# Rooms for expert weights reused in order of use, the split of x on VectorE, and splits behind the norm

## The chip, the cores and the metric

The kernel runs on one core of a Trainium2 chip. The metric is the device time of one execution in microseconds (us). Besides the executions that are only timed, one was taken with a profile; all durations below come from that one.

## The reference

The reference takes a sequence of 256 tokens of width 1024 in fp32 through two blocks of one kind, one block of another and a tail. Each of the three blocks ends in a mixture of 16 experts, of which a router picks two for each token. Cut to what matters here:

```
for l in range(2):                       # first kind of block
    h = concat(gla(x @ w_in), sgu(x @ w_in)) @ w_out
    x = layer_norm(ALPHA * x + h)
    h = cross_attention(x, mem)          # wq, wk, wv, wo
    x = layer_norm(ALPHA * x + h)        # the norm ahead of the router
    h = grouped_moe(x)
    x = layer_norm(ALPHA * x + h)
x = second_mixer(x)                      # attention and a scan
h = rms_norm(x)
x = x + hier_moe(h)
out = tail(x, p)                         # a gate, a projection of p, a norm

def moe(h):                              # both kinds, apart from the router
    out = 0
    for e in range(16):
        he = silu(h @ w_gate[e]) * (h @ w_up[e])      # 1024 -> 512
        out += combine[:, e] * (he @ w_down[e])       # 512 -> 1024
```

## The kernel before, in words

**Precision.** fp32 operands of most products are split in two parts: a high part (`xsh`, `whl`, `xTh`; a copy to the type fp32r on ScalarE, line 98) and a low part (`xsl`, `xTl`; the operand minus its high part, line 78 on VectorE). Experts' weights go to TensorE as they are.

**The norm ahead of the router** (`before_moe`). It works through the two halves of 128 tokens each (`tt` 0 and 1), in step with the projection that fills `x`. For each half: statistics and `rs` (line 103 on VectorE, then a power on GpSimd, line 104), turned pieces `zT` and the router's products `q`, the logits `lg`, the normalised `x` (`normal`), its high part `xsh` (`high`) and its low part `xsl` (`low`, line 360). `low` is a subtraction of 128x1024 on GpSimd. In the third block the normalised rows go to a tile `h`, and `rs` comes from squares summed on ScalarE. For the first two blocks a multiplication and an addition of gain and bias remain for each half (`finish`, four operations `x<-x,vec` on VectorE); `vec` is the tile that holds gain and bias.

**Routing and gathering** (`moe`). From the logits come the chosen experts (`sel`), each token's place in its expert's list (`pp` on TensorE, then `pos`), and matrices `Dm` of zeros and ones (`slots`, a comparison on VectorE: two of 128x256 for experts 0 to 3, then three of 128x512 for the others). `gath` multiplies `xsh` and `xsl` with `Dm`, 16 products each, into the tokens of four experts; `XG` is the copy out of PSUM, half of the pieces on ScalarE and half on VectorE. Then eight pairs of experts follow. In pair i TensorE runs gate (`gu`, 32 matmuls), up (`gu`), `dn` of pair i-1 (32 matmuls), and between these the sums `ysum`, two small gathers and two turns (`dtp`, `gut`). `mid` holds a pair's hidden values. The last pair's `dn` stands alone behind it.

**Weights and their rooms.** Each half of an expert's matrix is 1 MB and one DMA on SyncE's queue, written in program order (`expert_load`, line 214): per block 96 loads of four kinds' rooms. Four loads in a row are gate (or up, or down) of one pair: first half of expert 0, first half of expert 1, second half of expert 0, second half of expert 1. A load waits until the room it goes to has been read by TensorE; SyncE works in order, so what is behind it waits too. SyncE also has at most eight of these loads under way: each waits for the eighth before it.

Rooms are tiles of four pools: `raw` (7), `hl` (6), `t8` (9, shared with `Dm`, `XG`, `mid` and other activations) and `vec` (1). Before, the first pass takes n rooms of `t8`, then 7 `raw`, 6 `hl` and `vec` (n, called `flex`, is 4, 5 and 4 in the three blocks); later loads go round over the 7 `raw` and 6 `hl` alone. So the first load of the second round (load number 18, 19 and 18, counted from 0) takes the first `raw` room, which holds part of the first pair's up weights. `preload` issues the first 7+n loads while the stages ahead of the experts still run.

**The rest of what the change touches.** `rsqrt` has its first step on GpSimd unless `near` is set; `layer_norm` calls it without. `ahead` issues the loads of the next stage's weights at the end of a block, and splits the first few of them at once; `an` counts both. In the third block `fill` places the small projection of the tail (`ple_load` at the head, `ple_turn` with `ptp` in pair 0, `ple_proj` with 24 matmuls `plp` in pair 6). The instructions' order on each engine is fixed when the program is built, by a list scheduler that follows the program's order and the priorities given by `urgent` and `after`.

Of the kernel before, what the change touches and what calls it, by code (L numbers as in the profile page):

```python
# [6 lines left out]
F32 = mybir.dt.float32  # L7
# [12 lines left out]
CAP = 64  # L20
# [2 lines left out]


class Net:
    def __init__(self, tc, aps, cap=CAP, fallback=True, layers=2, bufs=(7, 6, 9, 2), flex=(4, 5, 4), late=2,
                 hp=("ln", "xm"), ao=1, plat=6, an=((2, 4), (3, 5), 3)):
        self.hp = hp
        self.ao = ao
        self.plat = plat  # L30
        self.an = an
        self.late = late
        self.flex = flex
        self.early = {}
# [158 lines left out]
    def preload(self, i, Wg, Wu, Wd):  # L193


        n = self.flex[i]
        self.rooms = ["t8"] * n + ["raw"] * self.NRAW + ["hl"] * self.NHL + ["vec"]
        self.loaded = 0
        todo = [(w, e, h) for p in range(2) for w in (0, 1) for h in range(2) for e in (2 * p, 2 * p + 1)]
        self.experts = {}  # L200
        for key in todo[:self.NRAW + n]:
            self.experts[key] = self.expert_load((Wg, Wu, Wd), *key)

    def expert_load(self, W, w, e, h):
        if self.loaded < len(self.rooms):
            room = self.rooms[self.loaded]
        else:
            m = (self.loaded - len(self.rooms)) % (self.NRAW + self.NHL)
            room = "raw" if m < self.NRAW else "hl"
        self.loaded += 1  # L210
        k, f = (8, 512) if w < 2 else (4, 1024)
        n = {"raw": self.NRAW, "hl": self.NHL, "t8": self.NT8, "vec": 1}[room]
        raw = self.sb.tile([128, k // 2, f], F32, tag=room, name="we", bufs=n)
        self.tc.keep_in_program_order(self.nc.sync.dma_start(
            raw, W[w][e].rearrange("(p k) f -> p k f", k=k)[:, h * (k // 2):(h + 1) * (k // 2), :]))
        return raw
# [64 lines left out]
    def layer_norm(self, x, l, i, at_once=False):  # L281
# [13 lines left out]
        def steps(tt, c, A):  # L295
# [14 lines left out]
            if at_once:  # L310
                self.ts(mv[:, 0:1], st[:, 0, 0:1], st[:, 0, 1:2], -1.0 / D, OP.add, OP.mult)
                tmp["first"] = self.ts(mv[:, 1:2], mv[:, 0:1], 0.03125, None, OP.mult).ins
                ss = self.sm("ss", [128, 1])
                self.act(r[1][:, :, tt * 128:(tt + 1) * 128], x[:, tt, :].rearrange("p (a b) -> p a b", a=KT), AF.Square,
                         scale=0.03125, bias=mv[:, 1:2], accum_out=ss)
                self.rsqrt(rs, ss, 1e-5)
            else:
                nc.vector.bn_aggr(mv, st)
                self.rsqrt(rs, mv[:, 1:2], 1e-5)
            for c in range(2):  # L320
                self.ts(o[c], o[c], mv[:, 0:1], rs, OP.add if at_once else OP.subtract, OP.mult)
                self.turn(r, x, tt, c, gb)
# [7 lines left out]
    def before_moe(self, x, rw, v, mean, keep, got):  # L330
# [26 lines left out]

        def low(tt):
            _, z, h, o = views(tt)
            nc.gpsimd.tensor_tensor(o, z, h.bitcast(F32), op=OP.subtract)  # L360

        def finish(tt):

# [7 lines left out]
        def steps(tt, c, A):  # L371
# [19 lines left out]
            if c == 0:  # L391
                if tt:
                    normal(0)
                    high(0)
                return
            rs[tt] = self.sm("rs", [128, 1])
            if mean:
# [14 lines left out]
            self.stt(lg[:, tt, :], p, rs[tt], B, OP.mult, OP.add)  # L412
            if tt == 0:
                return turned
            low(0)
            normal(1)

        def second(exp):
            with self.after(exp):
                h = high(1)  # L420
            low(1)
            if exp:
                with self.after(h):
                    self.warm()
        got.extend((lg, xs, second, (lambda: [finish(t) for t in range(2)]) if mean else None))
        return part

    def gain_cols(self, g, b=None):
# [421 lines left out]
    def moe(self, lg, xs, second, finish, gc, route, Wg, Wu, Wd, fill, source):  # L850
# [4 lines left out]
        W = Wg, Wu, Wd  # L855
        with self.urgent("rt"):
            sel, weights, exp = route(lg)
        second(exp)
# [15 lines left out]
        def gather(e, ks):  # L874
# [5 lines left out]
            with self.urgent("ga"):  # L880
# [7 lines left out]
                for k, p in ps.items():  # L888
                    for kk in (k, k + 1):
                        o, g = XG[e][:, kk], gain[:, kk:kk + 1]  # L890
                        if offset is None:
                            if kk % 2:
                                self.ts(o, p[:, kk - k], g, None, OP.mult)
                            else:
                                self.act(o, p[:, kk - k], AF.Copy, scale=g)
                        elif kk % 2:
                            self.ts(o, p[:, kk - k], g, offset[:, kk:kk + 1], OP.mult, OP.add)
                        else:
                            self.act(o, p[:, kk - k], AF.Identity, scale=g, bias=offset[:, kk:kk + 1])

        slots(0, 4, slice(0, 1))
        slots(0, 4, slice(1, 2))
        gather(0, (0, 2, 4, 6))
        for e in (4, 8, 12):
            last = slots(e, 4)
        gate = weights()
        if finish:
            with self.after(last.ins):
# [500 lines left out]
    def body(self, upto):  # L1409
# [94 lines left out]

        def fill(where):
            nonlocal ple
            if where == "head":
                ple = self.ple_load()
            if where == 0:
                ple = self.ple_turn(ple) + (ple,)  # L1510
            if where == self.plat:
                self.ple_proj(*ple)
# [32 lines left out]
```

## Time and profile before

| | us |
|---|---|
| median of 3 runs | 1478.57 (1477.70 to 1481.46) |
| profiled execution | 1477.46 |
| its span, first to last instruction | 1475.7 |
| TensorE busy | 1380.5 (94%) |
| VectorE busy | 631.3 (43%) |
| ScalarE busy | 505.0 (34%) |
| GpSimd busy | 80.3 (5%) |
| mean granted TensorE clock | 0.978 |

PE is TensorE's matmul side, DVE VectorE, ACT ScalarE, POOL GpSimd, SP SyncE; a `q` behind a name (SPq) is the engine's own queue of DMA issues and the like. In a timeline a row gives start, length, engine, line, operation, output and inputs, shape and count; a bracket gives how long the engine sat idle ahead of it, and what it waited for. Rows of several instructions give the time from the first one's start to the last one's end. The profiled execution lasts 1.8 us longer than its span and lies 1.1 us below the median.

### The profile page before, as it was taken

How to read it: one execution, taken by the hardware profiler on the slowest of the kernel's cores; microseconds unless marked ns; L12 is line 12 of the kernel's file. 1: busy time of each engine (PE TensorE's matmuls, PEld its weight loads, DVE VectorE, ACT ScalarE, POOL GpSimd, SP SyncE). 2: the span in 40 equal slices, each digit the busy share in tenths (PEclk: the TensorE clock that was granted, in tenths of full speed). 3: DMA queues.
4: the chain of work that ended last, by engine and by line, in shares of the span. 5: the costliest groups of instructions: out<-in, count | busy, mean ns of one | idle time of the engine just before them, and what ended most of it. 6: DMA issues, size and time to landing. Idle time of an engine off the chain costs nothing. (4 is left out here: it accounts for less than half of the span.)

```text
span 1475.7 us, 18102 instructions
## 1 busy us (share of the span) xinstructions
PE 1380.5 (94%) x7258; PEld 899.4 (61%) x7258; DVE 631.3 (43%) x1074; ACT 505.0 (34%) x784; POOL 80.3 (5%) x121
## 2 busy tenths in 40 slices
PE   8999998899988898999799998799999979999987
PEld 7889897444433686898444433499878864444335
DVE  5754754412111767763512110757676641212124
ACT  5634543111100474443211100458664440111122
POOL 2110001000000002000100000000000020000000
PEclk9999999899999999999899999899999989999998
DMA  9745428599999965328599999943534577999991
GB/s 336 273 167 179 164 87 352 203 421 421 421 419 421 341 222 173 117 98 346 203 393 420 421 421 420 352 131 117 197 120 140 204 316 294 421 421 421 418 389 44
DMA packets 101964, 421.50 MB, mean 286 GB/s; under 512 B 10676, under 2 KB 10896, under 8 KB 65008
## 3 DMA queue, kind: packets, MB, share of 16 engines
q1 hardware_dynamic: 97968, 409.17, 70.8%
q0 software_dynamic: 3904, 11.09, 2.4%
q8 instruction: 60, 0.98, 0.3%
q14 instruction: 32, 0.26, 0.0%
HBM read 419.18 MB, written 1.05 MB: 285 GB/s over the span
## 5 line engine op out<-in xcount | busy, mean ns | idle before, releaser
L64 PE MATMUL gu<-we,XG 128*64 128x512 f32 x1536 | 350.6, 596 | 3.9 <-DMA we<-in_w_gate_dram 1.7
L78 DVE TENSOR_TENSOR whl<-raw,whl 128x1024 fp32r<-128x1024 f32 (+1 forms) x210 | 241.1, 1163 | 146.9 <-ACT whl L98 138.2
L98 ACT ACTIVATE whl<-raw 128x1024 fp32r<-128x1024 f32 (+1 forms) x210 | 208.1, 1009 | 200.2 <-PE acc L64 97.6
L64 PEld LDWEIGHTS gu<-we,XG 128*64 128x64 f32 x1536 | 109.2, 137 | 210.0 <-issue 193.8
L64 PE MATMUL dn<-we,mid 128*64 128x512 f32 x768 | 181.6, 595 | 22.4 <-DMA we<-in_w_down_dram 20.3
L64 PE MATMUL acc<-whl,xTh 128*128 128x512 f32 (+2 forms) x640 | 194.4, 388 | 4.3 <-ACT xTh L98 3.4
L64 PEld LDWEIGHTS dn<-we,mid 128*64 128x64 f32 x768 | 57.8, 137 | 138.6 <-issue 94.6
L64 PEld LDWEIGHTS acc<-whl,xTh 128*128 128x128 f32 x640 | 119.9, 194 | 29.8 <-ACT xTh L98 4.0
L95 ACT ACTIVATE dh<-dn,gsl 128x512 fp32r<-128x512 f32 x42 | 28.8, 688 | 286.7 <-PE dn L64 286.7
L64 PE MATMUL facc<-xTh,whl 128*128 128x256 f32 x640 | 123.0, 288 | 1.8 <-ACT xTh L98 1.8
L64 PE MATMUL acc<-whl,xTl 128*128 128x512 f32 (+1 forms) x320 | 120.2, 385 | 0.1
L78 DVE TENSOR_TENSOR mid<-mid,gu 128x512 f32<-128x512 f32 x24 | 25.4, 1057 | 215.8 <-PE gu L64 215.8
L64 PEld LDWEIGHTS facc<-xTh,whl 128*128 128x128 f32 x640 | 102.7, 194 | 2.6 <-ACT xTh L98 2.0
L64 PE MATMUL facc<-xTl,whl 128*128 128x256 f32 x320 | 91.4, 287 | 0.0
L87 DVE SCALAR_TENSOR_TENSOR dl<-dn,gsl,dh 128x512 fp32r<-128x512 f32 x42 | 31.4, 750 | 134.6 <-ACT dh L95 132.1
L95 ACT ACTIVATE XG<-gath,gc 128x256 f32<-128x256 f32 x48 | 25.2, 535 | 134.9 <-PE gath L64 134.9
L64 PEld LDWEIGHTS acc<-whl,xTl 128*128 128x128 f32 x320 | 60.7, 193 | 12.4 <-DVE xTl L78 0.6
L92 DVE TENSOR_SCALAR XG<-gath,gc 128x256 f32<-128x256 f32 x32 | 16.9, 540 | 109.6 <-ACT XG L95 109.3
L64 PEld LDWEIGHTS facc<-xTl,whl 128*128 128x128 f32 x320 | 61.8, 193 | 0.7 <-issue 0.3
L64 PE MATMUL acc<-whl,oTh 128*128 128x512 f32 x160 | 49.5, 402 | 0.5 <-ACT oTh L98 0.5
L95 ACT ACTIVATE mid<-gu 128x512 f32<-128x512 f32 x24 | 14.3, 594 | 103.1 <-PE gu L64 103.1
L64 PEld LDWEIGHTS gath<-Dm,xsh 128*128 128x128 f32 x192 | 30.9, 222 | 28.6 <-issue 26.5
(366 smaller groups left out, 1769.8 us busy)
## 6 DMA issues: line engine op xcount, KB each, us to landing
we<-in_w_gate_dram SPq DMA_DIRECT2D x96, 1024.0 KB, 15.7
we<-in_w_up_dram SPq DMA_DIRECT2D x96, 1024.0 KB, 16.0
we<-in_w_down_dram SPq DMA_DIRECT2D x96, 1024.0 KB, 19.8
raw<-in_w_in_dram SPq DMA_DIRECT2D x38, 1024.0 KB, 8.7
raw<-in_w_out_dram SPq DMA_DIRECT2D x12, 1024.0 KB, 5.0
raw<-in_wk_x_dram SPq DMA_DIRECT2D x8, 1024.0 KB, 9.6
raw<-in_wv_x_dram SPq DMA_DIRECT2D x8, 1024.0 KB, 5.8
raw<-in_wq_x_dram SPq DMA_DIRECT2D x8, 1024.0 KB, 5.0
```

What stands on the lines that cost most here:

```text
L64: return self.nc.tensor.matmul(out, lhsT=l, rhs=r, start=start, stop=stop, skip_group_check=True)
L78: return self.nc.vector.tensor_tensor(out, a, b, op=op)
L87: return self.nc.vector.scalar_tensor_tensor(out, a, s, b, op0=op0, op1=op1, **k)
L92: return self.nc.vector.tensor_scalar(out, a, s1, s2, op0=op0, op1=op1)
L95: return self.nc.scalar.activation(out, a, f, **k)
L98: return self.nc.scalar.activation(out, a, AF.Copy)
```

## The change

Four things change.

1. *Rooms.* The first pass takes 2 `raw`, 1 `t8`, 4 `raw`, 1 `t8`, 1 `raw`, 6 `hl` and 1+t `t8`, with t (`flex`) now 1, 2 and 2: 17, 18 and 18 loads, all of them issued by `preload`. Later loads go round over 3 `raw`, `vec`, 4 `raw`, 6 `hl` and t `t8`: 15, 16 and 16 rooms. The first load of the second round now takes the room of load number 0, the first pair's first gate weights.
2. *The low part of x.* `low` is a subtraction on VectorE. `low(0)` follows `high(0)`; `low(1)` follows the second `Dm`. `finish` follows the last `XG` of the first gather, and the three large `Dm` follow the second small one.
3. *Norms.* `layer_norm` calls `rsqrt` with `near`, and no split is issued early by `ahead` (the loads are the same).
4. *The tail's projection.* `ple_load` stands in pair 5, `ple_turn` in pair 6 and `ple_proj` in pair 7.

```diff
-    def __init__(self, tc, aps, cap=CAP, fallback=True, layers=2, bufs=(7, 6, 9, 2), flex=(4, 5, 4), late=2,
-                 hp=("ln", "xm"), ao=1, plat=6, an=((2, 4), (3, 5), 3)):
+    def __init__(self, tc, aps, cap=CAP, fallback=True, layers=2, bufs=(7, 6, 9, 2), flex=(1, 2, 2), late=2,
+                 hp=("ln", "xm"), ao=1, plat=7, an=((0, 4), (0, 5), 0)):
...
-        n = self.flex[i]
-        self.rooms = ["t8"] * n + ["raw"] * self.NRAW + ["hl"] * self.NHL + ["vec"]
+        r, t = self.NRAW, self.flex[i]
+        self.rooms = ["raw"] * 2 + ["t8"] + ["raw"] * 4 + ["t8"] + ["raw"] * (r - 6) + ["hl"] * self.NHL + ["t8"] * (1 + t)
+        self.round = ["raw"] * 3 + ["vec"] + ["raw"] * (r - 3) + ["hl"] * self.NHL + ["t8"] * t
...
+        todo += [(2, e, h) for h in range(2) for e in range(2)]
...
-        for key in todo[:self.NRAW + n]:
+        for key in todo[:len(self.rooms)]:
...
-            m = (self.loaded - len(self.rooms)) % (self.NRAW + self.NHL)
-            room = "raw" if m < self.NRAW else "hl"
+        i = self.loaded
+        room = self.rooms[i] if i < len(self.rooms) else self.round[(i - len(self.rooms)) % len(self.round)]
...
-                self.rsqrt(rs, mv[:, 1:2], 1e-5)
+                self.rsqrt(rs, mv[:, 1:2], 1e-5, near=True)
...
-            nc.gpsimd.tensor_tensor(o, z, h.bitcast(F32), op=OP.subtract)
+            self.tt(o, z, h.bitcast(F32), OP.subtract)
...
                     high(0)
+                    low(0)
...
-            low(0)
             normal(1)
...
-            low(1)
...
         slots(0, 4, slice(0, 1))
-        slots(0, 4, slice(1, 2))
-        gather(0, (0, 2, 4, 6))
-        for e in (4, 8, 12):
-            last = slots(e, 4)
+        first = slots(0, 4, slice(1, 2)).ins
+        with self.after(first):
+            second[1]()
+        last = gather(0, (0, 2, 4, 6))
+        with self.after(first):
+            for e in (4, 8, 12):
+                slots(e, 4)
...
-            if where == "head":
+            if where == 5:
                 ple = self.ple_load()
-            if where == 0:
+            if where == 6:
                 ple = self.ple_turn(ple) + (ple,)
```

How the instructions move follows at three places. First VectorE in the first block, from the second half's `rs` to the first gather's copies. The rows of before, from the first `Dm` on (`den` and `gate` are the gates' norming):

```order
L78 TENSOR_TENSOR Dm<-iot,pos 128x256 x2
L78 TENSOR_TENSOR Dm<-iot,pos 128x2x256 x3
L818 RECIPROCAL den<-den 128x2
L78 TENSOR_TENSOR x<-x,vec 128x1024 x2
L78 TENSOR_TENSOR gate<-gate,den 128x32
L78 TENSOR_TENSOR x<-x,vec 128x1024 x2
L87 SCALAR_TENSOR_TENSOR go<-pos,gate 128x32
L92 TENSOR_SCALAR XG<-gath,gc 128x256
L78 TENSOR_TENSOR gparts<-gate,gparts 128x16x2
L92 TENSOR_SCALAR XG<-gath,gc 128x256 x3
```

The same stretch now:

```order
L78 TENSOR_TENSOR Dm<-iot,pos 128x256 x2
L78 TENSOR_TENSOR xsl<-x,xsh 128x1024
L78 TENSOR_TENSOR Dm<-iot,pos 128x2x256 x3
L816 RECIPROCAL den<-den 128x2
L78 TENSOR_TENSOR gate<-gate,den 128x32
L87 SCALAR_TENSOR_TENSOR go<-pos,gate 128x32
L78 TENSOR_TENSOR gparts<-gate,gparts 128x16x2
L92 TENSOR_SCALAR XG<-gath,gc 128x256 x2
L915 TENSOR_REDUCE cm<-cnt 128x1
L92 TENSOR_SCALAR XG<-gath,gc 128x256 x2
L78 TENSOR_TENSOR x<-x,vec 128x1024 x4
```

The subtraction of the second half came in behind the two small `Dm`, and the four operations of `finish` went from ahead of the copies `XG` to behind them. The first half's subtraction stands a little ahead of this, on the same engine, right behind the second half's `rs`:

```order
 L103 TENSOR_SCALAR rs<-mv 128x1
+L78 TENSOR_TENSOR xsl<-x,xsh 128x1024
+L87 SCALAR_TENSOR_TENSOR nr<-mv,rs 128x1
 L87 SCALAR_TENSOR_TENSOR lgt<-gwc,mv,q 128x16
-L87 SCALAR_TENSOR_TENSOR nr<-mv,rs 128x1
 L87 SCALAR_TENSOR_TENSOR lg<-lgt,rs,gwc 128x16
```

In the second block it stands one place later, behind `nr`, and there ScalarE has the fourth `zT` ahead of the first half's `xsh`, which was behind it. Second, ScalarE ahead of the router of the third block; `xsl,ss<-x` is the sum of squares, `re` the exponential that the gates need. Before:

```order
L95 ACTIVATE xsl,ss<-x 128x1024
L98 ACTIVATE zT<-trp 128x512
L95 ACTIVATE h_8537<-x,rs 128x1024
L98 ACTIVATE xsh<-h_8537 128x1024
L98 ACTIVATE zT<-trp 128x512 x2
L95 ACTIVATE xsl,ss<-x 128x1024
L98 ACTIVATE zT<-trp 128x512
L95 ACTIVATE h_8537<-x,rs 128x1024
L98 ACTIVATE xsh<-h_8537 128x1024
L95 ACTIVATE re<-re 128x40
L95 ACT_TABLE_LOAD
L95 ACTIVATE warm<-mhalf 128x1
```

And now:

```order
L98 ACTIVATE zT<-trp 128x512 x4
L95 ACTIVATE xsl,ss<-x 128x1024 x2
L95 ACTIVATE h_8537<-x,rs 128x1024 x2
L98 ACTIVATE xsh<-h_8537 128x1024
L95 ACTIVATE re<-re 128x40
L95 ACT_TABLE_LOAD
L95 ACTIVATE warm<-mhalf 128x1
L98 ACTIVATE xsh<-h_8537 128x1024
```

The first half's norm went behind the last `zT`, and the second `xsh` behind the table load. On VectorE of that block the first `xsl` now stands between `pos` and the first `Dm`, the second behind the last `Dm`. Third, TensorE at the end of the third block's experts, from the last pair's `dtp` on. The projection now stands there:

```order
L64 MATMUL gu<-we,XG 64x512 x16
L64 MATMUL dn<-we,mid 64x512 x16
L75 MATMUL dtp<-ident,pos 128x128 x4
L64 MATMUL plp<-whl,pT 128x512 x24
L75 MATMUL gut<-ident,mid 128x128 x4
L64 MATMUL dn<-we,mid 64x512 x16
```

`plp` came from the same place one pair earlier, ahead of the last pair's gate.

## Rows read from the trace of the kernel before

**Rows 1.** The page's head: the span, and busy time by engine.

```profile
span 1475.7 us, 18102 instructions
PE 1380.5 (94%) x7258; PEld 899.4 (61%) x7258; DVE 631.3 (43%) x1074; ACT 505.0 (34%) x784; POOL 80.3 (5%) x121
```

**Rows 2.** PE's waits by cause: us in total, times, longest.

```profile
PE dn L64 <- DMA we<-in_w_down_dram: 20.3, 17, 1.4
```

**Rows 3.** Timeline of PE: a pair's gate, the next pair's, and the blocks' ends.

```profile
338.47 7.09 PE L64 MATMUL gu<-we,XG 128*64 128x512 f32 x32
...
364.40 1.94 PE L64 MATMUL gu<-we,XG 128*64 128x512 f32 x8
...
483.88 7.12 PE L64 MATMUL dn<-we,mid 128*64 128x512 f32 x32 [0.69 <-ACT mid L98]
...
929.80 5.36 PE L64 MATMUL dn<-we,mid 128*64 128x512 f32 x22 [1.44 <-DMA we<-in_w_down_dram]
...
1391.10 4.47 PE L64 MATMUL plp<-whl,pT 128*128 128x512 f32 x18 [0.16 <-DVE dl L87]
...
1427.78 5.36 PE L64 MATMUL dn<-we,mid 128*64 128x512 f32 x22 [1.44 <-DMA we<-in_w_down_dram]
```

**Rows 4.** Stretches of 15 us: busy time by engine, clock, DMA share, GB/s.

```profile
270.00:285.00 15.00, 15.00 (x74) 5.54 (x71) 1.09 (x4) 1.05 (x2) 0.00 (x0) 1.00 0.33 118
...
435.00:450.00 15.00, 11.47 (x51) 3.96 (x52) 1.64 (x2) 1.16 (x2) 0.00 (x0) 1.00 1.01 422
```

**Rows 5.** Timeline of SP: the first load of each block's second round.

```profile
281.36 0.33 SPq L214 DMA_DIRECT2D we<-in_w_down_dram  x1
...
728.46 0.33 SPq L214 DMA_DIRECT2D we<-in_w_down_dram  x1
...
1225.80 0.33 SPq L214 DMA_DIRECT2D we<-in_w_down_dram  x1
```

**Rows 6.** Timeline of the first block's routing, all engines.

```profile
251.41 2.84 POOL L360 TENSOR_TENSOR xsl<-x,xsh 128x1024 fp32r<-128x1024 f32 x1 [3.75 <-ACT xsh L98]
251.86 0.15 DVE L103 TENSOR_SCALAR rs<-mv 128x1 f32<-128x1 f32 x1
254.22 0.54 POOL L104 TENSOR_TENSOR rs<-rs,mhalf 128x1 f32<-128x1 f32 x1
258.38 2.85 POOL L360 TENSOR_TENSOR xsl<-x,xsh 128x1024 fp32r<-128x1024 f32 x1 [3.62 <-ACT xsh L98]
261.65 3.88 PE L64 MATMUL gath<-Dm,xsh 128*128 128x256 f32 x16 [3.45 <-DVE Dm L78]
263.65 2.33 DVE L78 TENSOR_TENSOR x<-x,vec 128x1024 f32<-128x1024 f32 x2
265.33 2.48 PE L64 MATMUL gath<-Dm,xsl 128*128 128x256 f32 x16
269.52 2.80 PE L64 MATMUL gu<-we,XG 128*64 128x512 f32 x12 [0.36 <-DVE XG L92]
```

**Rows 7.** `Dm` in the first and the third block: ns min/median/max, first and last start.

```profile
L78 DVE TENSOR_TENSOR Dm<-iot,pos x5: 410/677/3041, 258.5 to 263.0; 128x512 fp32r<-128x512 f32 x3, 128x256 fp32r<-128x256 f32 x2
...
L78 DVE TENSOR_TENSOR Dm<-iot,pos x5: 416/681/683, 1207.5 to 1209.4; 128x512 fp32r<-128x512 f32 x3, 128x256 fp32r<-128x256 f32 x2
```

**Rows 8.** Timeline of the routing in the second and the third block.

```profile
701.96 0.23 DVE L87 SCALAR_TENSOR_TENSOR lg<-lgt,rs,gwc 128x16 f32<-128x16 f32 x1
...
716.60 3.65 PE L64 MATMUL gu<-we,XG 128*64 128x512 f32 x16 [0.26 <-DVE XG L92]
...
1201.94 2.04 ACT L98 ACTIVATE xsh<-h 128x1024 fp32r<-128x1024 f32 x1
...
1208.08 3.84 PE L64 MATMUL gath<-Dm,xsh 128*128 128x256 f32 x16 [0.83 <-DVE Dm L78]
...
1213.96 2.37 PE L64 MATMUL gu<-we,XG 128*64 128x512 f32 x10
```

**Rows 9.** The page's groups: a strided product on VectorE.

```profile
L78 DVE TENSOR_TENSOR mid<-mid,gu 128x512 f32<-128x512 f32 x24 | 25.4, 1057 | 215.8 <-PE gu L64 215.8
```

More of the change, by code (lines that the diff above doesn't have):

```diff
@@ L193, in preload @@
     def preload(self, i, Wg, Wu, Wd):
-        n = self.flex[i]
-        self.rooms = ["t8"] * n + ["raw"] * self.NRAW + ["hl"] * self.NHL + ["vec"]
+        r, t = self.NRAW, self.flex[i]
+        self.rooms = ["raw"] * 2 + ["t8"] + ["raw"] * 4 + ["t8"] + ["raw"] * (r - 6) + ["hl"] * self.NHL + ["t8"] * (1 + t)
+        self.round = ["raw"] * 3 + ["vec"] + ["raw"] * (r - 3) + ["hl"] * self.NHL + ["t8"] * t
         self.loaded = 0
         todo = [(w, e, h) for p in range(2) for w in (0, 1) for h in range(2) for e in (2 * p, 2 * p + 1)]
+        todo += [(2, e, h) for h in range(2) for e in range(2)]
         self.experts = {}
-        for key in todo[:self.NRAW + n]:
+        for key in todo[:len(self.rooms)]:
             self.experts[key] = self.expert_load((Wg, Wu, Wd), *key)
     def expert_load(self, W, w, e, h):
-        if self.loaded < len(self.rooms):
-            room = self.rooms[self.loaded]
-        else:
-            m = (self.loaded - len(self.rooms)) % (self.NRAW + self.NHL)
-            room = "raw" if m < self.NRAW else "hl"
+        i = self.loaded
+        room = self.rooms[i] if i < len(self.rooms) else self.round[(i - len(self.rooms)) % len(self.round)]
         self.loaded += 1
@@ L315, in steps @@
                          scale=0.03125, bias=mv[:, 1:2], accum_out=ss)
-                self.rsqrt(rs, ss, 1e-5)
+                self.rsqrt(rs, ss, 1e-5, near=True)
             else:
                 nc.vector.bn_aggr(mv, st)
-                self.rsqrt(rs, mv[:, 1:2], 1e-5)
+                self.rsqrt(rs, mv[:, 1:2], 1e-5, near=True)
             for c in range(2):
@@ L424, in second @@
                     self.warm()
-        got.extend((lg, xs, second, (lambda: [finish(t) for t in range(2)]) if mean else None))
+        got.extend((lg, xs, (second, lambda: low(1)), (lambda: [finish(t) for t in range(2)]) if mean else None))
         return part
@@ L857, in moe @@
             sel, weights, exp = route(lg)
-        second(exp)
+        second[0](exp)
         pp = self.rp([128, 2, 16], "pp")
@@ L890, in gather @@
                         o, g = XG[e][:, kk], gain[:, kk:kk + 1]
[L891 to L897, printed above, removed]
-                        else:
-                            self.act(o, p[:, kk - k], AF.Identity, scale=g, bias=offset[:, kk:kk + 1])
+                        b = None if offset is None else offset[:, kk:kk + 1]
+                        if kk % 2:
+                            last = self.ts(o, p[:, kk - k], g, b, OP.mult, None if b is None else OP.add)
+                        else:
+                            self.act(o, p[:, kk - k], AF.Copy if b is None else AF.Identity, scale=g,
+                                     **({} if b is None else {"bias": b}))
+            return last
         slots(0, 4, slice(0, 1))
-        slots(0, 4, slice(1, 2))
-        gather(0, (0, 2, 4, 6))
-        for e in (4, 8, 12):
-            last = slots(e, 4)
+        first = slots(0, 4, slice(1, 2)).ins
[5 more added lines that the diff above has]
+                slots(e, 4)
         gate = weights()
```

## The prediction

> **What bounds the kernel now.** TensorE is busy for 94% of the span [rows 1], so time can only come from its gaps or its slow stretches. The list of its waits was read first: the largest entry, 20.3 us in 17 waits, is `dn` waiting for down weights [rows 2], and it shows that the experts' stages are short of weights. How much is lost there follows from a pair's pace. Unhurried, one pair follows the other after 364.40 - 338.47 = 25.9 us [rows 3], so eight take 207.4. From the first `gu` to the end of the last `dn` the three blocks took 491.0 - 269.5 = 221.5, 935.2 - 716.6 = 218.6 and 1433.1 - 1214.0 = 219.1, the last with some 6.0 of `plp` (4.47 for 18 of its 24 matmuls) [rows 3, 6, 8]. So 14.1, 11.2 and 5.7 us are lost, 31 in all. The stretches tell why: from 270 to 285 TensorE is full while DMA brings 118 GB/s, and from 435 to 450 DMA is full at 422 GB/s while TensorE works 11.47 of 15 us [rows 4]. DMA needs 2.49 us for a load of 1 MB at that rate, 29.8 for the 12 of a pair, against 25.9 on TensorE; it lives on its lead, and stands idle at the beginning, where the lead could be built. The cause of that is the row of SP: the first load of the second round is issued at 281.36, 728.46 and 1225.80 [rows 5], each time 11.8 to 11.9 us behind the first `gu`, when the first half of the pair's up weights has been read.
>
> The other gaps lie in the routing, where everything waits in a chain; the timelines were read for it [rows 6 to 8].
>
> **The change part by part: the start of the experts.** *First block.* (a) GpSimd's first `xsl` (2.84) stands from 251.41 to 254.25, and the power that makes `rs`, whose input was ready at 252.01, comes right behind it at 254.22 [rows 6]. Now VectorE does that subtraction behind `rs`. Its length is not shown. The lower bound is 1.17, a contiguous operation of this size (2.33 for two `x<-x,vec` [rows 6]); the upper 2.1, twice the strided product of 512 columns at 1.06 [rows 9]. I take 1.8, nearer the strided row, since ScalarE too takes 2.04 for `xsh` in this layout [rows 8]. It ends at 253.8, with the power done beside it: 0.5 us sooner than before, between 1.1 sooner and 0.2 later. (b) The second `xsl` on GpSimd starts at 258.38, and the first `Dm` (start 258.5) takes 3.04 us instead of 0.41, the length that the other one of its form has [rows 6, 7]. In the third block, with no subtraction beside it, the longest `Dm` is 0.68 [rows 7]. So 2.63 go. The second subtraction now follows two `Dm` of 0.41 and has 3.88 us of `gath<-Dm,xsh` to hide behind; if that cover were gone it would cost its 1.8. (c) `gath` ends at 267.81 and `gu` begins 1.71 later, behind a copy `XG` on VectorE that stood behind `finish` (four `x<-x,vec`, two of them from 263.65) [rows 6]. Third block, no `finish`: `gu` follows the copies much sooner. I take 1.2 for this, of at most 1.6. `finish` then runs under the first `gu`; it frees `vec` some 6 us after the start, which is ahead of the fourth load of the second round, the one that needs it. Sum 0.5 + 2.6 + 1.2 = 4.3 sooner, from 3.2 to 5.3.
>
> *Second block.* (b) and (c) are the same, 2.6 and 1.2 to 1.5. But ScalarE there makes the first `xsh` behind the fourth `zT`, and VectorE the subtraction ahead of `lgt` and `lg`: `lg`, at 701.96 before [rows 8], comes near 703.3. Sum 2.6 + 1.3 - 1.4 = 2.5 sooner, from 1.5 to 3.2.
>
> *Third block.* Here the new order costs. The first half's norm and `xsh` stand behind the second half's squares, `re`, a table load and `warm` stand ahead of the second `xsh`, which ended at 1203.98 before [rows 8] and will end near 1210.2. The first `gath<-Dm,xsh` needs both halves; it began at 1208.08 [rows 8]. So the start comes about 2.0 us later, from 0 (if ScalarE's earlier parts are all hidden) to 3.5.
>
> Here the Trainium skill weighs in twice, and no number above needs it. By "VectorE: DVE Perf Modes", section on TRN2 errata, a two-input fp32 operation takes (N + 151) cycles at 0.96 GHz, 1.22 us for 1024, and its section on the 1× mode says that strides don't matter; by that each subtraction costs 0.6 less and the start in the first two blocks comes 0.6 sooner still. Rows 9 speaks against it, with 1.06 us for 512 columns where the formula gives 0.69. By "SBUF — State Buffer", section "Who interferes with whom", a two-input VectorE operation and a GpSimd one that reads SBUF exclude each other, whichever starts first. Rows 7 agrees for `Dm`; the same rule would now hold the power back behind the subtraction in the first block, and (a) would be 0.2 later instead of 0.5 sooner. Both ends lie inside the bounds.
>
> **The rooms.** A gate's half takes 7.09 / 2 = 3.55 us [rows 3], so the second round's first load is now issued 3.55 behind the first `gu`. *First block*: at 269.5 - 4.3 + 3.55 = 268.8, 12.6 sooner. One load more is left for it (17 rooms, not 18), 2.5 us: every later landing comes 10.1 sooner. TensorE alone would end at 265.2 + 207.4 = 472.6, while DMA's pace gives 491.0 - 10.1 = 480.9, so DMA still decides: -10.1. *Second block*: 714.1 + 3.55 = 717.7, 10.8 sooner, less 2.5 for a load more: -8.3, to 926.9, still above TensorE's 921.5. *Third block*: 1216.0 + 3.55 = 1219.5, 6.3 sooner with as many rooms as before. Now TensorE decides: 1216.0 + 207.4 + 6.0 = 1429.4 against 1433.1, at best -3.7. Moving `plp` takes its 6 us of cover from the sixth pair's `dn` and puts them ahead of the last `dn`, where loads are latest. The load on TensorE is the same, and I leave 1.7 of waiting: -2.0, from -4 to +2.
>
> The round has a `t8` room now, and its slot last held the first pair's `mid`. That load, number 31, is due at 268.8 + 14 × 2.49 = 303.7, but `dn` of the first pair ends near 306, so it and all behind it in SP's order wait some 2 us. Eight loads under way cover part of it: +1.0 in the first block, nothing in the others, whose slot comes two loads later. Upper bound 2.5 each.
>
> **Edits with one answer.** `near` moves a step of 128x1 from GpSimd to VectorE, where a row of its kind takes 0.15 [rows 6]; the uncalled early splits end up in nearly the same order on ScalarE. Together 0, within 0.6 either way. The normal loads of the preload come no later, since they still wait for the stage ahead.
>
> **Sum.** -10.1 + 1.0 - 8.3 - 2.0 = -19.4. The profiled 1477.5 becomes 1458.1; the profile lies 1.1 below the median of 1478.57, so the forecast is 1459.2, say 1459. Bounds: with every start at its best, no `t8` wait and -4 in the third block about -26; with starts at their worst, `t8` waits of 2.5 and +2 about -9. So 1452 to 1470.
>
> **The rivals.** *A: only the start counts.* If the experts' last stretch is paced by something else that the lead doesn't reach (the 11 us of 31 that the waits for down weights don't name), the loads' lead is worth nothing: -4.3 - 2.5 + 2.0 = -4.8, 1473.8. For it: only 20.3 of 31 are named. Against: DMA is full for that whole stretch [rows 4]. *B: the shared rooms make activations and weights wait for each other.* A `t8` room of the round passes between weights and `mid` or `XG`; SP stops at a load whose slot is still held, and ScalarE at a `mid` whose slot holds weights that have not been read. There are five or so such turns in a block, fifteen in all. At 1.3 us of TensorE's time each the 19.4 are gone; at 2 us the kernel takes 1478.6 - 19.4 + 30 = 1489. Against it: a slot is handed on behind work that lies a pair back, and eight loads are queued. *C: more than forecast.* If TensorE also runs closer to its own pace in the second block and the third keeps its early start: -28, 1450. *D: the edit on splits does nothing* as the order says; it is in the forecast at 0.
>
> **How the numbers follow.** Forecast 0.72 (1452 to 1470), A 0.14 (1471 to 1477), B 0.07, C 0.07 (below 1452). About 0.3%, 4.4 us, is what a measurement of this kernel can tell from no change. Faster by more: the forecast, C and half of A, 0.86. Within it: the other half of A and 0.01 of B, 0.08. Slower: 0.06. The range takes in the forecast and part of C and A: 1450 to 1471.
>
> **What would show it.** In the new profile: the first load of the second round 3.5 to 4 us behind each block's first `gu`; no stretch of 15 us near 118 GB/s there; `Dm` never above 0.7; the first `gu` at about 265.2; the first block's `dn` ending near 482; the waits for down weights well below 20.3. `mid` waiting for a load, or SP waiting for ScalarE or VectorE between 300 and 480 for more than a few us, would show B. A first `gu` that is earlier with an end of `dn` earlier by no more than that would show A.

## The result, and the profile after

| us | before | changed |
|---|---|---|
| median | 1478.78 (1477.70 to 1481.46, 4 runs) | 1461.84 (1460.11 to 1464.28, 4 runs) |
| profiled execution, its span | 1477.46, 1475.7 | 1460.11, 1458.3 |
| TensorE busy | 1380.5 | 1375.7 |

The ratio is 0.9884, with a 95% interval from 0.9862 to 0.9906: the kernel became 1.2% faster, 16.9 us by the medians and 17.4 by the profiled spans. The forecast was 1459, from 1450 to 1471. A second series of the changed kernel gave 1461.63 (1460.03 to 1463.04).

Where the time went is best read from anchors that both timelines have: a block's last `x` ahead of its router, the first `gu`, and the end of the last `dn`. Each line is the time from the anchor before it; a second execution of the changed kernel and three of the experiments stand beside it.

| us | before | changed | changed, second execution | rooms alone | all but rooms | flex 1, 1, 1 |
|---|---|---|---|---|---|---|
| block 1: start to last x | 250.2 | 250.0 | 250.3 | 249.5 | 250.6 | 250.7 |
| last x to first gu | 19.4 | 14.7 | 14.6 | 19.9 | 15.4 | 15.3 |
| experts | 221.5 | 217.3 | 215.0 | 215.8 | 221.5 | 216.6 |
| block 2: to last x | 206.2 | 207.9 | 207.1 | 207.3 | 207.2 | 206.6 |
| last x to first gu | 19.4 | 17.1 | 17.1 | 20.6 | 15.4 | 14.6 |
| experts | 218.6 | 214.9 | 215.0 | 215.2 | 218.6 | 211.1 |
| block 3: to last x | 262.8 | 261.1 | 263.8 | 264.2 | 263.5 | 260.0 |
| last x to first gu | 16.0 | 17.2 | 17.3 | 18.7 | 14.4 | 15.9 |
| experts | 219.2 | 216.0 | 215.7 | 215.7 | 219.5 | 214.5 |

The two executions of the changed kernel differ by 2.3 us in the first block's experts and by 2.7 us on the way to the third block's last `x`. A difference of that size in one of these stages can't be put down to an edit.

PE's waits by cause in the changed kernel (us in total, times, longest) answer to [rows 2]:

```profile
PE dn L64 <- DMA we<-in_w_down_dram: 13.9, 11, 2.0
...
PE gath L64 <- DVE Dm L78: 5.3, 3, 3.6
```

The waits for down weights fell from 20.3 us in 17 waits to 13.9 in 11; they did not go away, and the longest grew from 1.4 to 2.0. The timeline of the first block's routing answers to [rows 6]:

```profile
251.79 1.99 DVE L78 TENSOR_TENSOR xsl<-x,xsh 128x1024 fp32r<-128x1024 f32 x1
252.01 2.12 POOL L104 TENSOR_TENSOR rs<-rs,mhalf 128x1 f32<-128x1 f32 x1 [4.43 <-DVE rs L103]
254.50 0.23 DVE L87 SCALAR_TENSOR_TENSOR lg<-lgt,rs,gwc 128x16 f32<-128x16 f32 x1
258.00 0.76 DVE L78 TENSOR_TENSOR Dm<-iot,pos 128x256 fp32r<-128x256 f32 x2
258.57 3.88 PE L64 MATMUL gath<-Dm,xsh 128*128 128x256 f32 x16 [0.83 <-DVE Dm L78]
258.68 2.03 DVE L78 TENSOR_TENSOR xsl<-x,xsh 128x1024 fp32r<-128x1024 f32 x1
262.24 2.15 PE L64 MATMUL gath<-Dm,xsl 128*128 128x256 f32 x16
264.68 7.09 PE L64 MATMUL gu<-we,XG 128*64 128x512 f32 x32 [0.23 <-DVE XG L92]
265.52 4.62 DVE L78 TENSOR_TENSOR x<-x,vec 128x1024 f32<-128x1024 f32 x4
```

Both `Dm` of 128x256 together take 0.76 where the first alone took 3.04; `gath` of `xsh` hides the second `xsl`; `finish` lies under the first `gu`. And GpSimd's power, 0.54 before, lasts 2.12: it starts 0.22 behind VectorE's `xsl` and ends 0.35 behind it.

SP's issues of the first loads of the second round, of the three blocks, answer to [rows 5]:

```profile
268.36 3.78 SPq L213 DMA_DIRECT2D we<-in_w_down_dram  x3
...
710.74 0.80 SPq L213 DMA_DIRECT2D we<-in_w_down_dram  x2
...
1203.82 0.81 SPq L213 DMA_DIRECT2D we<-in_w_down_dram  x2
```

They come 3.68 us behind each first `gu` (264.68, 707.06, 1200.14) instead of 11.8 to 11.9.

Routing of the third block, against [rows 8]; all engines:

```profile
1189.08 2.03 ACT L98 ACTIVATE xsh<-h 128x1024 fp32r<-128x1024 f32 x1
1191.00 0.23 ACT L95 ACTIVATE re<-re 128x40 f32<-128x40 f32 x1
1191.25 1.28 ACT L95 ACT_TABLE_LOAD   x1
1192.66 2.05 ACT L98 ACTIVATE xsh<-h 128x1024 fp32r<-128x1024 f32 x1
1193.68 0.55 PE L64 MATMUL gath<-Dm,xsh 128*128 128x256 f32 x1 [3.65 <-DVE Dm L78]
1194.76 3.33 PE L64 MATMUL gath<-Dm,xsh 128*128 128x256 f32 x15 [0.52 <-ACT xsh L98]
```

The gather starts and then waits for the second `xsh`, which stands behind the table load, as the order said.

The shared `t8` room of the round is met first at load 31 of the first block. SP's wait there, from 295 to 310:

```profile
SPq L213 <- PE dn L64: 6.5, 1, 6.5
```

The load is issued at 305.8, when `dn` of the first pair has ended, and lands 4.9 us behind the one before it instead of 2.5.

Last, a place that nothing in the forecast named. SP and DMA in the second block's fourth pair: the timeline of SP, its waits from 775 to 800, and two stretches of 5 us (columns as in [rows 4]):

```profile
779.70 14.74 SPq L213 DMA_DIRECT2D we<-in_w_up_dram  x4
```

```profile
SPq L213 <- PE gu L64: 17.8, 2, 13.0
```

```profile
785.00:790.00 5.00, 5.00 (x29) 2.29 (x29) 0.54 (x1) 0.56 (x1) 0.00 (x0) 1.00 1.02 423
790.00:795.00 5.00, 5.00 (x26) 1.67 (x24) 1.06 (x1) 0.00 (x0) 0.00 (x0) 1.00 0.43 143
```

SP stands still for 13.0 us, and DMA, after it has worked off what was queued, drops to 143 GB/s. The load is number 49 of the block, counted from 0, and goes to a `t8` slot. SP goes on at 793.16, when the fourth pair's up ends (at 793.1); of the `t8` tiles that gate and up read, only the `XG` of the third and fourth pair is in use until then, so the slot held this `XG`. In the third block SP's wait is as long, 13.0 us.

### The profile page after: what moved, and what is told of

The parts are those of the page before. It is cut to its first block, busy times and chain, and to the rows that moved or that the text cites. A ratio compares the mean times of both kernels' runs of the same rounds, so it can differ in the third digit from the quotient of the medians.

```text
span 1458.3 us, 18050 instructions
## 1 busy us (share of the span) xinstructions
PE 1375.7 (94%) x7258; PEld 899.7 (62%) x7258; DVE 636.3 (44%) x1088; ACT 504.8 (35%) x784; POOL 63.7 (4%) x107
## 5 line engine op out<-in xcount | busy, mean ns | idle before, releaser
L64 PE MATMUL gu<-we,XG 128*64 128x512 f32 x1536 | 347.0, 596 | 4.2 <-DMA we<-in_w_up_dram 1.9
L64 PE MATMUL dn<-we,mid 128*64 128x512 f32 x768 | 179.3, 599 | 16.0 <-DMA we<-in_w_down_dram 13.9
L92 DVE TENSOR_SCALAR XG<-gath,gc 128x256 f32<-128x256 f32 x32 | 17.1, 543 | 100.6 <-ACT XG L95 100.2
L64 PEld LDWEIGHTS gath<-Dm,xsh 128*128 128x128 f32 x192 | 30.7, 221 | 27.0 <-issue 17.1
## 6 DMA issues: line engine op xcount, KB each, us to landing
we<-in_w_up_dram SPq DMA_DIRECT2D x96, 1024.0 KB, 11.8
```

What stands on the lines that cost most here:

```text
L64: return self.nc.tensor.matmul(out, lhsT=l, rhs=r, start=start, stop=stop, skip_group_check=True)
L92: return self.nc.vector.tensor_scalar(out, a, s1, s2, op0=op0, op1=op1)
```

## The experiments

All compare with the kernel before, measured beside them (medians 1478.69 to 1479.35).

### The parts apart

**Rooms alone.** The kernel before, with

```diff
-                 flex=(4, 5, 4) ... plat=6
+                 flex=(1, 2, 2) ... plat=7
-        self.rooms = ["t8"] * n + ["raw"] * self.NRAW + ["hl"] * self.NHL + ["vec"]
+        self.rooms = ...   # as changed, with round, todo and the places of ple
```

> The kernel before with the new rooms and the tail's projection moved (the two were left together, since the new rooms need it), nothing else. Theory (rooms and starts act separately, as in the forecast's sum): the three experts' stages, from the first gu to the end of the last dn, shorten as in the changed kernel, by 3 to 4.5 us each, 11 in all, and the starts stay where they were, so 1478.6 - 11 = about 1467 to 1468. Rival A (the lead is worth nothing, only the start counts): within 2 us of 1478.6. Second rival (the two edits need each other: finish frees vec too late or the copies are late, so the lead only counts with the early start): less than 5 us.

Measured: 1471.77, ratio 0.9955 (0.9938 to 0.9971), so 6.9 us less. The experts shorten by 5.7, 3.4 and 3.5 us, but the routing gets longer by 0.5, 1.2 and 2.7: the rooms alone also bring the new order on ScalarE in the second and third block. The lead is worth its time without the early start, so rival A is out; the 11 us that were expected are more than the 6.9 that came, because they left out what the rooms do to the routing.

**All but the rooms.** The changed kernel with the `preload` and `expert_load` of before and `flex` 4, 5, 4.

> The changed kernel with the rooms of before (order of rooms, flex and preload), everything else as changed. Theory: starts 4.7 and 2.3 us sooner in the first two blocks and later in the third, with DMA then the limit: what the weights don't allow is lost again. The first load of the second round follows the start, so landings come sooner by the same; about 1478.6 - 5 to -7 = 1472 to 1474. Rival (the start is free time that the late weights eat): within 3 us of 1478.6. The 1.7 us that the second block loses between the first block's sums and its own last x come with the splits behind the norm, so they are here too if that edit is their cause, and not in the run with rooms alone.

Measured: 1469.90, ratio 0.9944 (0.9927 to 0.9961), so 8.8 less. The routing takes 15.4, 15.4 and 14.4 us, 4.0, 4.0 and 1.6 less than before, and the experts 221.5, 218.6 and 219.5, as before to 0.3 us. The early starts are kept in full, since the second round's first load follows the first `gu`. In the third block the routing became 1.6 shorter, and ScalarE has the order of before there: the later start of the third block comes with the rooms, not with the subtractions and norms. The two halves add up to 15.7 of the 16.9.

**The subtractions back on GpSimd**, in their new places:

```diff
-            self.tt(o, z, h.bitcast(F32), OP.subtract)
+            nc.gpsimd.tensor_tensor(o, z, h.bitcast(F32), op=OP.subtract)
```

> The changed kernel with the two subtractions xsl back on GpSimd, in the program's new places (behind the first high, behind the second Dm). Theory (GpSimd's subtraction and VectorE's two-operand work stop each other): Dm or whatever two-operand operation of VectorE lies beside the 2.84 us grows by up to 2.6, the second gather part waits for xsl, and the starts come 1 to 2.5 us later in each of the first two blocks: 1463 to 1467. Rival (the gain of the starts comes from finish behind the copies alone): within 1 us of the changed kernel.

Measured: 1465.19 (1463.13 to 1470.10), ratio 0.9903 (0.9886 to 0.9919). From last `x` to first `gu` each block takes 18.7 us, against 14.7, 17.1 and 17.2. Timeline of GpSimd and VectorE, and the durations of `Dm` (ns min/median/max), first block:

```profile
253.72 2.84 POOL L359 TENSOR_TENSOR xsl<-x,xsh 128x1024 fp32r<-128x1024 f32 x1
253.77 2.80 DVE L87 SCALAR_TENSOR_TENSOR nr<-mv,rs 128x1 f32<-128x1 f32 x1 [0.72 <-POOL rs L104]
...
259.99 2.85 POOL L359 TENSOR_TENSOR xsl<-x,xsh 128x1024 fp32r<-128x1024 f32 x1 [3.44 <-ACT xsh L98]
260.25 5.01 DVE L78 TENSOR_TENSOR Dm<-iot,pos 128x256 fp32r<-128x256 f32 x5
263.27 3.87 PE L64 MATMUL gath<-Dm,xsh 128*128 128x256 f32 x16 [3.28 <-DVE Dm L78]
```

```profile
L78 DVE TENSOR_TENSOR Dm<-iot,pos x5: 411/679/2870, 260.3 to 264.6; 128x512 fp32r<-128x512 f32 x3, 128x256 fp32r<-128x256 f32 x2
```

The first subtraction holds up VectorE's `nr`, which takes 2.80 instead of 0.16, and beside the second one a `Dm` is stretched to 2.87 again, until GpSimd is through. Put back, this edit costs 4.0, 1.6 and 1.5 us in the three blocks of the profiled execution. That one, 1470.10, is the longest of the four; by the medians the kernel is 3.4 us slower than the changed one. That is the rule of the Trainium skill ("SBUF — State Buffer", section "Who interferes with whom": a two-input VectorE operation and a GpSimd one that reads SBUF exclude each other, whoever starts first), and this pair of runs shows it both ways: GpSimd's `xsl` stretches `Dm` from 0.41 to 2.87, and in the changed kernel VectorE's `xsl` stretches GpSimd's power from 0.54 to 2.12.

**`finish` ahead of the copies again**:

```diff
-        last = gather(0, (0, 2, 4, 6))
+        gather(0, (0, 2, 4, 6))
...
-                slots(e, 4)
+                last = slots(e, 4)
```

> The changed kernel with finish behind the three large Dm as before, so that it stands ahead of the copies XG again (three of its four operations ahead of the first copy on VectorE). Theory (the forecast's term c): from the last x to the first gu 1.2 to 1.6 us more in the first two blocks, nothing in the third; 1463 to 1465. Rival (the copies are waited for on ScalarE anyway): within 0.5 us of 14.7 and 17.1.

Measured: 1471.14 (1470.22 to 1473.17), ratio 0.9949 (0.9934 to 0.9964): 9.5 us slower than the changed kernel beside it (1461.63), where 1.2 to 1.6 us in each of two blocks were expected. Timeline of VectorE and PE, first block:

```profile
262.44 2.34 DVE L78 TENSOR_TENSOR x<-x,vec 128x1024 f32<-128x1024 f32 x2
...
264.80 1.22 DVE L78 TENSOR_TENSOR x<-x,vec 128x1024 f32<-128x1024 f32 x1
...
265.94 0.99 DVE L92 TENSOR_SCALAR XG<-gath,gc 128x256 f32<-128x256 f32 x2
266.53 0.19 PE L64 MATMUL cnt<-sel,oneb 128*128 128x16 bf16 x2 [2.15 <-DVE XG L92]
```

Three of the four operations stand ahead of the copies, and TensorE waits 2.15 for them. The routing takes 17.1, 18.8 and 17.3, so 2.4 and 1.7 more, and nothing in the third block: the mechanism holds, at the price of 1.2 to 1.6 that was too low. Another 5 us are outside of it. From the end of a block to the next block's last `x` it takes 210.8 and 263.9 (changed kernel: 207.9, 261.1), at a mean granted clock of 0.97 and 0.96 instead of 0.98 and 0.97, which would be some 2 and 3 us, an estimate. The order of other work changed too (ScalarE's `whl` and TensorE's `acc` and `facc` stand elsewhere in the third block's mixer), so these 5 us were not traced to one cause.

### What the shared rooms cost

**No `t8` in the round**:

```diff
-        self.round = ["raw"] * 3 + ["vec"] + ["raw"] * (r - 3) + ["hl"] * self.NHL + ["t8"] * t
+        self.round = ["raw"] * 3 + ["vec"] + ["raw"] * (r - 3) + ["hl"] * self.NHL
```

> The changed kernel without the t8 rooms in the round (14 rooms in each block: 3 raw, vec, 4 raw, 6 hl); the first pass is as changed. In the trace of the changed kernel SP waits 13 us for load 49 in the second and third block, its slot held by XG of the third and fourth pair until their last gate and up weights are read, and DMA drops to 143 GB/s for 5 us. Theory (that wait is where the second block's 2 us went): the gap in DMA goes, and the second and third block's experts end 1 to 2.5 us sooner, the first one's 0 to 1.5: 1457 to 1460. Rival (two rooms fewer cost more than the wait): the same as the changed kernel or up to 3 us slower, with the load stalls of the last pairs growing.

Measured: 1464.96, from 1456.05 to 1469.08, ratio 0.9915 (0.9899 to 0.9932). The profiled execution is the shortest; in it the experts take 215.5, 213.9 and 215.8 (changed: 217.3, 214.9, 216.0). The gap at 790 is gone:

```profile
785.00:790.00 5.00, 5.00 (x26) 1.59 (x24) 0.00 (x0) 0.00 (x0) 0.00 (x0) 1.00 1.01 418
790.00:795.00 5.00, 5.00 (x26) 1.72 (x24) 1.06 (x1) 0.00 (x0) 0.00 (x0) 1.00 1.02 421
```

So the wait for the slot was real, and without it the second block's experts are 1.0 shorter; the 1.8 of the first block are less than what two executions of the changed kernel differ by there, and the third block's 0.2 is nothing. Over all runs the kernel is no better than the changed one, as the rival said. Of the runs, the longest had the lowest mean clock (0.972, against 0.979 in the shortest).

**One `t8` instead of two**, `flex` 1, 1, 1:

```diff
-    def __init__(..., flex=(1, 2, 2), ...
+    def __init__(..., flex=(1, 1, 1), ...
```

> The changed kernel with flex 1, 1, 1: one t8 room fewer in the first pass and in the round of the second and third block (17 loads first, 15 rooms round). In the order, ScalarE of the second block has xsh ahead of the fourth zT again. Theory (the routing got longer because the weights took the t8 slots that the activations ahead of the router use): from the last x to the first gu the second block takes 14.7 instead of 17.1, the third 15 to 16 instead of 17.2; the room less costs the second and third block's experts up to 2.5 us each; 1458 to 1463. Rival (VectorE's xsl itself is the cost): 17 in the second block.

Measured: 1449.91 (1447.11 to 1450.28), ratio 0.9797 (0.9784 to 0.9811): 11.7 us faster than the changed kernel beside it, below the 1458 to 1463 that were expected, and, level with two variants of it below (1450.68 and 1451.02), the best found. The routing is 15.3, 14.6 and 15.9 as expected. What was not expected is that a room less makes the experts faster: 211.1 and 214.5 us in the second and third block, 3.9 and 1.2 less than in the run of the changed kernel beside it (215.0 and 215.7). The 11.7 us are not all routing and experts: 3.8 of them lie on the way to the third block's last `x` (260.0 against 263.8 beside it), at a mean granted clock of 0.99 against 0.97, and 1.0 behind the last block; neither was traced. The mean GB/s of DMA in 40 equal parts of the second block's experts, of the changed kernel and of this one:

```profile
GB/s 23 396 424 424 291 428 421 427 421 421 419 424 416 419 430 279 279 424 425 425 416 419 427 421 421 421 418 421 417 424 419 419 424 422 422 417 413 426 401 387
```

```profile
GB/s 33 399 430 422 292 426 418 424 422 422 416 422 419 422 422 418 422 419 421 422 418 421 422 422 422 418 422 422 415 421 418 422 422 422 421 422 421 419 402 387
```

The two parts of 279 in the first are the wait for `XG`; with one room the second turn is load 46, which SP issues at 771.25, 0.1 behind the one before it, so its slot was free, and the gap isn't there. Which tile that slot had held was not read. Two parts of 5.4 us at 279 instead of 421 are 3.6 us of DMA time (an estimate), near the 3.9 that the experts gained.

**Neither**: `flex` 1, 1, 1 and no `t8` in the round.

> As the run before, and no t8 room in the round (17 loads first, 14 rooms round). Theory: the early starts of the run before and no wait of SP for a slot of XG or mid; the experts' stages of the second and third block as long as without t8 in the round (213.9 and 215.8) or up to 2 longer; 1456 to 1461. Rival (each room less costs its 2.5 us of lead): 1461 to 1465.

Measured: 1461.05 (1456.39 to 1462.98), ratio 0.9866 (0.9850 to 0.9882). The number fits the rival, but the rows don't: a room less costs 4.6 us in the second block's experts (215.6 against 211.1) and nothing in the others (215.9 and 214.8), and 10.1 us are lost between the first block's end and the second's last `x` (216.7 against 206.6). At the beginning of it PE waits, by the timeline, for the sum on VectorE, and VectorE for TensorE's queue at line 1043, the branch that is taken when an expert has more tokens than places:

```profile
491.49 1.88 DVE L87 SCALAR_TENSOR_TENSOR x<-x,ysum 128x512 f32<-128x512 f32 x3 [5.84 <-PEq L1043]
492.23 1.22 PE L64 MATMUL acc<-whl,mTh 128*128 128x512 f32 x2 [6.39 <-DVE x L87]
```

With one `t8` room in the round the two waits are 1.10 and 0.87. VectorE and ScalarE work in the same order there in both kernels. Over the whole way the mean granted clock is 0.95 instead of 0.98, and over the second block's experts 0.98 instead of 1.00. So this run doesn't tell what the round without `t8` is worth: a wait at a branch and a lower clock hide it, and why the branch took longer in this execution stays open.

**Rooms alone at `flex` 1, 1, 1**: the kernel of the first experiment with `flex=(1, 1, 1)`.

> The kernel before with the new rooms at flex 1, 1, 1 and the tail's projection moved; subtractions, norms and splits as before. Theory (additive parts): the routing as before (19.4, 19.4, 16.0 from the last x to the first gu), the experts' stages as with flex 1 in the changed kernel (216, 211 to 212, 214.5 to 215), so 5.5 + 7 + 4.5 = 17 us less than before, 1461 to 1463; the rooms alone then give most of what the whole change gave. Rival (flex 1 helped only by way of the routing): 1466 to 1470.

Measured: 1463.57 (1460.87 to 1464.64), ratio 0.9892 (0.9877 to 0.9907), so 15.7 less than before and 8 less than with `flex` 1, 2, 2. Experts 215.4, 211.0 and 214.7; routing 19.9, 19.9 and 16.5, as before to 0.6. The theory holds, at the upper end of its 1461 to 1463: with a single shared room the rooms alone give nearly what the whole change gave.

### The rest

**Both subtractions behind the second `Dm`**, with `flex` 1, 1, 1:

```diff
                     high(0)
-                    low(0)
...
-        got.extend((lg, xs, (second, lambda: low(1)), ...
+        got.extend((lg, xs, (second, lambda: [low(0), low(1)]), ...
```

> The kernel with flex 1, 1, 1, and both subtractions xsl behind the second Dm instead of one behind the first high. In the changed kernel the first xsl (1.99 us on VectorE, with GpSimd's power stretched from 0.54 to 2.12 beside it) stands on the way from rs to lg. Theory (that xsl costs its 2 us ahead of the router, while gath<-Dm,xsh of 3.88 us hides two subtractions of 2.0): from the last x to the first gu 13 to 13.5 instead of 15.3, 14.6 and 15.9, that is 1.3 to 2.5 us less in each block, 1444 to 1447. Rival (the three large Dm, now 2 us later on VectorE, delay the gates and the copies): 14.5 to 15.5, 1448 to 1450.

Measured: 1451.02 (1447.44 to 1451.92), ratio 0.9796 (0.9783 to 0.9809): no gain. Routing 15.5, 15.1 and 17.1. Timeline of GpSimd, VectorE and PE, first block:

```profile
252.57 0.54 POOL L104 TENSOR_TENSOR rs<-rs,mhalf 128x1 f32<-128x1 f32 x1 [4.43 <-DVE rs L103]
...
258.65 3.97 DVE L78 TENSOR_TENSOR xsl<-x,xsh 128x1024 fp32r<-128x1024 f32 x2
262.22 2.82 PE L64 MATMUL gath<-Dm,xsl 128*128 128x256 f32 x16
262.53 1.89 DVE L78 TENSOR_TENSOR Dm<-iot,pos 128x512 fp32r<-128x512 f32 x3
264.87 0.54 DVE L92 TENSOR_SCALAR XG<-gath,gc 128x256 f32<-128x256 f32 x1
```

The power is short again and `lg` comes 0.6 sooner behind the last `x`, but the two subtractions fill the whole of `gath`'s first part, the large `Dm` come behind them, and the copies wait. The 2 us moved and came back as another wait, as the rival said.

**Early splits again**, with `flex` 1, 1, 1: `an=((2, 4), (3, 5), 3)`.

> The kernel with flex 1, 1, 1 and the early splits of ahead as before (2, 3 and 3 of them). The order of instructions differs from it in two places of the third block's end only. Theory (the edit moves nothing): within 2 us of the kernel with flex 1, 1448 to 1451. Rival (early splits hold up the norm): 2 to 5 us slower.

Measured: 1450.68 (1446.73 to 1451.94), ratio 0.9806 (0.9791 to 0.9821): the edit on the splits moves nothing that can be measured, as forecast at D.

**The changed kernel again.**

> The changed kernel once more, for the spread: its time moves with the granted clock's falls (in its profile TensorE stands at half clock from 620 to 628 where the kernel before did from 631 to 635, 1.7 us lost). Theory: 1460 to 1464, and the runs with a lower mean clock are the longer ones. In the profile the second block's way from the first block's last dn to its own last x is 206.2 as before or 207.9, depending on such a fall. Rival (that 1.7 comes from the order of the splits behind the norm): 207.9 without a longer fall of the clock.

Measured: 1461.63, ratio 0.9883 (0.9868 to 0.9899). From the first block's end to the second's last `x` it took 207.1, the first time 207.9. Stretches of 10 us (TensorE's clock is the third number from the end) of the first profile, then of this one:

```profile
610.00:620.00 10.00, 10.00 (x63) 8.68 (x62) 8.07 (x15) 7.33 (x14) 0.56 (x1) 1.00 0.65 234
620.00:630.00 10.00, 8.75 (x54) 8.65 (x54) 8.52 (x14) 2.48 (x5) 0.43 (x1) 0.66 0.56 211
```

```profile
610.00:620.00 10.00, 9.46 (x67) 8.44 (x65) 8.13 (x18) 7.11 (x14) 0.55 (x1) 1.00 0.61 211
620.00:630.00 10.00, 9.23 (x65) 9.23 (x66) 7.40 (x10) 3.17 (x4) 1.15 (x2) 0.83 0.67 261
```

TensorE's clock has two levels here, 2.4 and 1.2 GHz, and a mean of 0.66 or 0.83 says that part of the stretch ran at the lower one. The same program, with the same wait of 1.2 to 1.3 us for `xTh` ahead of it, lost 3.4 us of clock (10 × 0.34, an estimate) in one execution and 1.7 in the other. The kernel before, with a wait of 1.33 there, has 0.83 from 630 to 640, the same loss as the second execution, and took 206.2. So about half of the 1.7 us that the second block seemed to lose ahead of its router, 0.8, went with the clock; the other 0.9 was there in both executions and was not traced.

## Why the prediction held, point by point

**The start of the experts** was forecast 4.3 and 2.5 us sooner and 2.0 later. Measured from the last `x`: 4.7 and 2.3 sooner, 1.2 later. (a) `xsl` takes 1.99 on VectorE, near the upper bound of 2.1; I took 1.8. The price of 1.22 that the prediction took from the Trainium skill did not come; what that page ("VectorE: DVE Perf Modes", section on the 1× mode) says is that odd strides work in this mode, not what they cost. The power did not run beside the subtraction but was held until it ended, and `nr` waited 0.39 for it, so `lg` came 0.2 sooner from the last `x`, not 0.5: the text had given 0.5 sooner and, by the rule named above from the Trainium skill, 0.2 later (0.5 less the power's 0.54 would have been no change); the measurement lies between, and the hold on the power is what that rule says. (b) The 2.6 us of `Dm` are gone as reckoned. (c) `gu` follows `gath` by 0.3 (264.68 - 264.39) instead of 1.71, 1.4 where 1.2 was taken; the experiment puts `finish` at 1.7 to 2.4. In the third block the second `xsh` came at 1192.66, 9.7 us behind the last `x`, and the gather did stop for it. In this execution the last `x` itself came 1.7 sooner from the block before, in the second one 1.0 later, so that offset is luck.

**The rooms** were forecast at -4.8 (with 1.0 for the `t8` wait), -5.8 and -4.0 for the experts' stages, the start's share taken off. Measured: -4.2, -3.7 and -3.2, and in the second execution -6.5, -3.6 and -3.5. In the first block the two executions lie on either side of the forecast; what is missing in both is the second block's share. The direction, the place of the first load (3.55 reckoned, 3.68 measured) and DMA as the limit were right. The step that failed is "nothing in the others, whose slot comes two loads later". It followed only the first turn of the `t8` room, load 31 or 33. In the second and third block the second turn, load 49, takes a slot that holds `XG` until the fourth pair's up is read; SP stood still for 13 us and DMA lost about 3.6. At load 31 the price was too low: 2.4 (a landing 4.9 behind the one before, not 2.5) where 1.0 was taken, still inside the bound of 2.5.

A second term was put at nothing without a reason: that every later landing moves by as much as the first one, so that DMA's gaps behind it stay as they were. In the second block 76 loads landed from 733.6 to 929.8 before, 77 from 716.0 to 916.5 in the changed kernel, and 78 from 712.7 to 909.4 with one shared room. Less 2.49 for each, the gaps are 7.0, 8.8 and 2.5 us. With them the sum comes out: -5.8 + 1.8 = -4.0 for the changed kernel (-3.7 measured). With one room the first load comes 8.2 us sooner behind the first `gu` and two loads more are left, 5.0, so the forecast's way gives -3.2; with 4.5 less of gaps it is -7.7 (-7.5 measured). Taking rooms in the order of their use closes gaps, and two shared rooms opened others.

**Rival B** was given 0.07 as a slower kernel. Its mechanism, SP stopped at a room that an activation still holds, is what happened, in two blocks of three and at a price of some 4 and 1 us in the experts instead of 30, about a quarter of what the gain would have been without it. The sign named for it, SP waiting for ScalarE or VectorE, would have missed it: SP waited for TensorE to have read `XG`.

**Rival A** fell: all but the rooms gave 8.8 us, the rooms alone 6.9, and neither eats the other. But the sum had split the gain as 4.8 and 14.6. The delays that it charged to the start of the second and third block come with the rooms: without the new rooms the routing takes 15.4, 15.4 and 14.4 us, and the rooms alone lengthen it by 0.5, 1.2 and 2.7. The total was nearly right, the shares of the two parts were not.

**The sum.** Forecast -19.4, profile -17.4: the start gave 1.0 more than forecast (0.4 more, 0.2 less, 0.8 more), the rooms 3.5 less (0.6, 2.1, 0.8), and what lies between and behind the blocks nearly evens out (+1.7, -1.7, -0.5). So the median is within 3 us of the forecast, part of it by luck: a start that was taken too low made up for 1.0 of the 3.5 that the rooms lacked. Of the bounds, the better one of about -26 is not what its terms give: -11.1, -9.0 and -4 are -24.1. The claim that no stretch would stay near 118 GB/s held: the first 15 us behind the first `gu` now have 276, 273 and 275.

## What to carry to other kernels

When weights that stream in go round over rooms, ask of each room who read it last before the load, in every turn and not only in the first: one room whose last reader comes late stops the whole queue behind it, and a room less can be faster. Reusing rooms in the order of their use pays as soon as a stream runs at its limit later, because the idle time of its beginning can't be made up. Work that a second engine takes over for nothing may stop the first one, as GpSimd's `xsl` did here; the longest instance of an operation beside its shortest, 3.04 us against 0.41, shows it.

## What the runs showed that was not expected

- TensorE's clock is part of a comparison of 1%. Behind the same wait of 1.2 to 1.3 us the same program ran at a mean of 0.66 or of 0.83 of full clock for 10 us, so 3.4 or 1.7 us lost, and its runs spread over 4 us, 1460.11 to 1464.28; of one experiment's four runs the one with mean clock 0.979 took 1456 and the one with 0.972 took 1469.
- Fewer waits for weights (11 instead of 17) were longer ones (2.0 instead of 1.4 us at most).
- A power on 128x1 on GpSimd took 2.12 us instead of 0.54 because VectorE was subtracting beside it; with the subtraction moved behind the second `Dm` it took 0.54 again.
- A subtraction of 128x1024 whose input is read with a stride takes 1.99 to 2.03 us on VectorE, against 1.17 for a contiguous operation of that size [rows 6], and 2.84 on GpSimd.
